# A decoder block on one core: y's row in PSUM from the first norm on, and compressed scores at a group's last unit

## The chip, the cores and the metric

The kernel runs on one core of a Trainium2 chip. The metric is the device time of one execution in microseconds; a kernel's time is the median of its runs. TensorE (PE) multiplies matrices, VectorE (DVE) and GpSimd (POOL) work element by element, ScalarE (ACT) applies functions and copies, SyncE (SP) and POOL start transfers (DMA). SBUF is the memory on the chip that all of them read; PSUM is the smaller one, in banks of 512 float32 words a partition, into which PE writes and from which DVE and ACT read.

## The reference

One layer of a decoder for 256 tokens (T) of width 2048 (D), in float32:

```python
h = x @ w_in                                     # q, 6 groups of kv columns, gates, conv columns
o_nsa  = nsa_group(q, ...)                       # 16 heads in 4 groups, head size 64
o_conv = conformer_conv_group(conv_ab, ...)      # 31 taps, norm, silu
mix = concatenate([o_nsa, o_conv], -1) @ w_out
x   = layer_norm(DN_ALPHA * x + mix, ln1_g, ln1_b)
x   = layer_norm(DN_ALPHA * x + peer_ffn(x, ...), ln2_g, ln2_b)
```

`nsa_group` adds three attentions with a gate each: over 15 compressed blocks of keys (32 tokens each, 16 apart), over selected blocks of 64 tokens (with 256 tokens there are 4 blocks, and up to 16 would be taken, so it is causal attention), and over a window of 512 (causal attention again, with keys of its own). All have a bias by distance.

`peer_ffn` computes, for each token and each of 8 heads, two score rows `s1` and `s2` over 128 keys, takes the best 16 of each, the best 16 of their 256 sums, and with those 16 experts out of 16384 the sum of softmax weight x gelu(y . u_e) x v_e:

```python
h = gelu(einsum('btd,bthkd->bthk', yb, u_tab[eidx]))
out = einsum('bthk,bthkd->btd', softmax(top) * h, v_tab[eidx])
```

## The kernel before

**Matmuls in three.** A float32 product is made of three matmuls on halves of the numbers: `hi` is the operand rounded by an ACT copy (L234), `lo` = operand - hi is a subtraction on DVE or POOL (L252), and `mm3` (L290 to L293) adds up x_hi w_hi, x_hi w_lo and x_lo w_hi, so that in the profile a weight block stands for rows of L291, L292 and L293. Weights come in pieces of 2048 columns a partition (`raw`, four buffers), each split in two halves (`hi57_0` is the first half of piece 57).

**Stages, by the time in the trace.** Up to 200 us the input projection, the convolution and the compression of keys. From 200 to 375 us the attention, beside the last query columns (`pq1` to `pq3`, one piece of `w_in` for each group of heads) and the output mix. From 375 to 405 us the first norm, whose result is `y`. From 405 to 505 us the wq stage: the router's matmuls `pwq0` to `pwq7`, a head each (four weight halves, 96 matmuls of 256 columns), with the keys' scores (`ps`), the search for the best 16 and the first ten experts. From 505 to 980 us the stage of the first dense pass: PE multiplies y with a table `u` of all experts in the lower columns (`ut` are transposes, `hp` the products), while POOL gathers (L1163) the upper 1024 columns of the chosen rows of `u` one expert for 128 tokens at a time, and DVE takes their dot product with y's upper row (`dot`, L1174). Then comes a stage of masks, from 1145 us on the v table in the same manner, and the last norm.

**What sets the order around the attention.** The order on each engine is written out by a planner. `run` (L268) issues the pieces' matmuls and moves a `clock` by a hand-made cost for each. Generators wait in `streams`; after every block of matmuls `advance` steps those whose time has come. The attention is one such generator. It goes over 16 units `u` (two heads of a group `g = u // 4` by 128 query tokens); `per` is 4. For a unit it issues `scores` (L776; `s01` and `s11` are heads 0 and 1, query tokens 128 to 255), then ACT's exponentials (`powers`, L801), the normalisation by DVE (`weigh`, L809 to L813), transposes by PE (`turn`, L824; `t00`, `t10`) with a copy by ACT (L827), and the sum over the values (`combine`), each in the round of a later unit. The compressed scores of a group (`compressed`, L714: matmuls `cs`, DVE's `csb`, transposes `ct`) run as a side generator: for group 0 ahead of the loop, for group g + 1 in the round of the first unit of group g (L901: `if u % per == 0`), which waits there for the flag `q{g+1}`, set when `pq{g+1}` is complete. Four times in each round `share` (L872) says when to go on: a list of `goals` holds, for each step, how much of the matmul work that was left at the start is to be spent by then.

**Where things lie around the first norm.** PSUM holds 8 banks. The pool `psa` has the accumulators with the tags a0 to a3, `psb` the tags S, T and o. `acc_tile` (L189) hands out accumulators by turns over four banks, or over two while the flags say so (then a2 and a3 serve `turn_tile`, L198, for the attention's transposes). In the wq stage accumulators turn over all four. y's upper row `yg` lies in SBUF. After the wq stage `apsum.close()` gives up `psa` and `psb`, and a pool `psy` takes two banks for `yp`, into which ACT copies `yg` for tokens 0 to 127 (L1447). `dot` multiplies with `yg` until then and with `yp` from then on (`yrow`). The ten dots in the wq stage therefore read `yg`. The first three tiles of `ut` are made in the wq stage (`u_split(n, True)`, L1225) in banks of the accumulators.

On POOL the wq stage's queue is, over and over: four subtractions `lo` of 128 x 1024 (L252), then a few gathers.

## Time and profile before

| | |
|---|---|
| median of 3 runs | 1660.19 us (1659.75 to 1663.21) |
| the profiled execution | 1663.05 us |
| its span in the trace | 1661.3 us |
| PE's mean granted clock in it | 0.992 |
| busy: PE, DVE, POOL, ACT | 98%, 87%, 55%, 49% |
| weight loads (PEld) | 90% |
| transfers | 475.19 MB, 286 GB/s over the span |

The span runs from the first to the last instruction; what lies around it is 1.75 us in this execution. The profile names a group of instructions by line, engine, operation, output <- input (buffer numbers left out) and how often (x). In a view by order of time a row is start, duration, engine, line and names, and a bracket gives the time that the engine stood still ahead of it and what ended that. In a view by stretches the count behind each busy time is the number of instructions. A granted clock of 1.00 is full speed of PE, 0.50 half of it.

### The profile page before, as it was taken

The page shows a single profiled execution, that of the slowest core. Times are in us where ns is not written, and L with a number is a line of the kernel's source. Part 1 is how long each engine was busy: PE and PEld are TensorE (multiplying, and loading weights), DVE is VectorE, ACT ScalarE, POOL GpSimd, SP SyncE. Part 2 cuts the span into 40 slices and gives each one's busy share as a digit, 9 for nine tenths or more (in the row PEclk, how much of TensorE's full clock was granted, in tenths as well). Part 3 has the DMA queues.
Part 4 walks back from the last instruction along what each step waited for, and adds up shares of the span by engine and source line. Part 5 has one row for each costly group of instructions (what it writes and reads, how often), then busy time and mean ns, then how long its engine had stood idle before and what let it go on. Part 6 is the DMA issues. An engine that isn't in the chain of part 4 may idle for free.

```text
span 1661.3 us, 30634 instructions
## 1 busy us (share of the span) xinstructions
PE 1621.6 (98%) x11627; PEld 1501.5 (90%) x11627; DVE 1449.5 (87%) x2651; ACT 813.4 (49%) x1261; POOL 909.0 (55%) x662
## 2 busy tenths in 40 slices
PE   9999999999999999999999999989999999999996
PEld 9998988988989999999999997878888888888885
DVE  6999668756799999999999879878898999989998
ACT  4445756544424444444444546867444444444442
POOL 1875000064783333333333347848887887778883
PEclk9999999999999999999999999999999999999998
DMA  9774535365648999999999988765999999999997
GB/s 290 234 232 130 173 102 179 110 232 191 228 159 313 349 350 354 349 351 346 350 349 355 358 314 268 244 217 169 332 358 357 352 358 349 356 347 359 363 355 260
DMA packets 178348, 475.19 MB, mean 286 GB/s; under 512 B 18304, under 2 KB 86424, under 8 KB 177944
## 3 DMA queue, kind: packets, MB, share of 16 engines
q1 hardware_dynamic: 117188, 253.62, 45.0%
q0 software_dynamic: 57488, 218.66, 35.9%
q8 instruction: 91, 1.49, 0.4%
q10 hardware_dynamic: 3524, 0.95, 0.3%
q14 instruction: 57, 0.47, 0.1%
HBM read 468.32 MB, written 4.85 MB: 285 GB/s over the span
## 4 chain that ended last, share of the span: by engine, by line
PE 61%; DVE 17%; DMA 13%; ACT 4%; issue 3%; POOL 1%; SPq 0%; POOLq 0%; DVEq 0%; ACTq 0%
DMA vr<-in_peer_v_dram 11%; PE hp L293 7%; PE hp L291 7%; PE hp L292 7%; PE ut L1231 6%; PE bank L1635 3%; PE bank L1682 3%; DVE gu L1174 3%; DVE vl L1744 3%; ACT vh L1743 3%; DVE gacc L1710 2%; PE f L292 2%; PE f L293 2%; PE f L291 2%; DVE taps L485 2%
## 5 line engine op out<-in xcount | busy, mean ns | idle before, releaser
L1705 POOL DMA_INDIRECT gv<-in_peer_v_dram,e x256 | 399.5, 1560 | 98.8 <-DVE gacc L1710 52.5
L1163 POOL DMA_INDIRECT gu<-in_peer_u_dram,eu x206 | 195.8, 951 | 311.7 <-DVE gu L1174 229.6
L291 PE MATMUL hp<-yh,uh 128*128 128x256 f32 x1024 | 310.4, 303 | 0.4 <-ACT W L1482 0.3
L1743 ACT ACTIVATE vh<-vr 128x1408 fp32r<-128x1408 f32 x127 | 175.6, 1382 | 276.1 <-DVE gacc L1710 241.5
L293 PE MATMUL hp<-yh,ul 128*128 128x256 f32 x1024 | 290.2, 283 | 0.9 <-DVE ul L1235 0.9
L292 PE MATMUL hp<-yl,uh 128*128 128x256 f32 x1024 | 289.2, 282 | 0.0
L292 PE MATMUL f<-vl,wh 128*128 128x512 f32 (+1 forms) x768 | 288.2, 375 | 1.0 <-DVE vl L1744 1.0
L293 PE MATMUL f<-vh,wl 128*128 128x512 f32 (+1 forms) x768 | 287.8, 375 | 1.0 <-DVE wl L1733 1.0
L291 PE MATMUL f<-vh,wh 128*128 128x512 f32 (+1 forms) x768 | 288.1, 375 | 0.0
L1234 ACT ACTIVATE uh<-ut 128x512 fp32r<-128x512 f32 x256 | 152.8, 598 | 254.7 <-PE ut L1231 210.1
L252 POOL TENSOR_TENSOR lo<-raw,hi 128x1024 fp32r<-128x1024 f32 (+1 forms) x84 | 189.1, 2268 | 134.7 <-ACT hi L234 128.5
L1744 DVE TENSOR_TENSOR vl<-vr,vh 128x1408 fp32r<-128x1408 f32 x127 | 206.3, 1625 | 43.2 <-ACT vh L1743 38.9
L1174 DVE SCALAR_TENSOR_TENSOR gu<-gu,yp 128x1024 f32<-128x1024 f32 x196 | 232.6, 1212 | 0.4 <-ACT yp L1457 0.2
L234 ACT ACTIVATE hi<-raw 128x1024 fp32r<-128x1024 f32 (+1 forms) x137 | 141.4, 1036 | 146.3 <-PE pwq L292 30.2
L1710 DVE SCALAR_TENSOR_TENSOR gacc<-gv,hv,gacc 128x640 f32<-128x640 f32 x246 | 206.7, 879 | 3.9 <-DMA gv<-in_peer_v_dram,e 3.8
L293 PEld LDWEIGHTS hp<-yh,ul 128*128 128x128 f32 x1024 | 195.5, 191 | 1.4 <-DVE ul L1235 1.1
L291 PEld LDWEIGHTS hp<-yh,uh 128*128 128x128 f32 x1024 | 196.0, 191 | 0.8 <-ACT W L1482 0.8
L292 PEld LDWEIGHTS hp<-yl,uh 128*128 128x128 f32 x1024 | 196.5, 192 | 0.0
L1235 DVE TENSOR_TENSOR ul<-ut,uh 128x512 fp32r<-128x512 f32 x256 | 166.8, 681 | 14.9 <-ACT uh L1234 12.9
L292 PEld LDWEIGHTS f<-vl,wh 128*128 128x128 f32 x768 | 148.5, 193 | 23.3 <-DVE vl L1744 2.5
L293 PEld LDWEIGHTS f<-vh,wl 128*128 128x128 f32 x768 | 148.6, 194 | 21.2 <-DVE wl L1733 1.4
L291 PEld LDWEIGHTS f<-vh,wh 128*128 128x128 f32 x768 | 148.5, 193 | 20.6
(410 smaller groups left out, 3556.2 us busy)
## 6 DMA issues: line engine op xcount, KB each, us to landing
vr<-in_peer_v_dram SPq DMA_DIRECT2D x128, 704.0 KB
ur<-in_peer_u_dram SPq DMA_DIRECT2D x128, 512.0 KB
raw<-in_w_in_dram SPq DMA_DIRECT2D x32, 1024.0 KB
raw<-in_w_out_dram SPq DMA_DIRECT2D x16, 1024.0 KB
raw<-in_peer_wq_dram SPq DMA_DIRECT2D x15, 1024.0 KB
gv<-in_peer_v_dram,e POOLq DMA_INDIRECT x256
gu<-in_peer_u_dram,eu POOLq DMA_INDIRECT x206
raw<-in_w_in_dram SPq DMA_DIRECT2D x4, 608.0 KB
```

Of the source, the lines that this page charges most:

```text
L252: e.tensor_tensor(lo[:, a:b], src[:, a:b], hi[:, a:b].bitcast(F32), op=OP.subtract)
L291: nc.tensor.matmul(acc, lhsT=ah, rhs=bh, start=start, stop=False)
L292: nc.tensor.matmul(acc, lhsT=ah, rhs=bl, start=False, stop=False)
L293: nc.tensor.matmul(acc, lhsT=al, rhs=bh, start=False, stop=stop)
L1163: nc.gpsimd.indirect_dma_start(out=gt, out_offset=None, in_=ug, in_offset=bass.IndirectOffsetOnAxis(ap=fl(eu, tt)[:, c:c + 1], axis=0))
L1174: nc.vector.scalar_tensor_tensor(gt, gt, 1.0, yr, op0=OP.mult, op1=OP.mult, accum_out=hv[:, tt, c:c + 1])
L1234: nc.scalar.activation(uh, pt, AF.Copy)
L1235: nc.vector.tensor_tensor(ul, pt, uh.bitcast(F32), op=OP.subtract)
L1705: nc.gpsimd.indirect_dma_start(out=gvs[j, tt], out_offset=None, in_=v_tab, in_offset=bass.IndirectOffsetOnAxis(ap=fl(e4, tt)[:, j:j + 1], ...
L1710: engine.scalar_tensor_tensor(gacc[:, tt], gvs.pop((j, tt)), wv[:, tt, j:j + 1], gacc[:, tt], op0=OP.mult, op1=OP.add)
L1743: nc.scalar.activation(vh, src[:, s], AF.Copy)
L1744: (nc.gpsimd if early else nc.vector).tensor_tensor(vl, src[:, s], vh.bitcast(F32), op=OP.subtract)
```

## The change

It has two parts.

In the **attention**, the side generator of the next group's compressed scores starts in the round of a group's last unit (u = 3, 7, 11) where it started in that of its first (u = 0, 4, 8), and it waits for the queries' copy (`box["qt"]`) besides the flag. `share` no longer takes from a list made at the start: at each step it shares what is left of the matmul work at that time by the weights still to come.

In **PSUM**, the accumulators a2 and a3 move to a pool of their own on the right side (`psc`), which is closed when the first norm is done. `psy` and `yp` are opened there at once, with the copy and the setting of `yrow`, which were behind the wq stage. With the flag "norm" set, the wq stage's accumulators turn over two banks, and its three early `ut` tiles take the tags T, o and T of `psb`.

```diff
+    cpsum = ctx.enter_context(ExitStack())
+    psc = cpsum.enter_context(tc.tile_pool(name="psc", bufs=1, space=PSUM, side="right"))
...
     def acc_tile(name):
-        two = "kv" in flags and "attn" not in flags
+        two = ("kv" in flags and "attn" not in flags) or "norm" in flags
...
-        return psa.tile([P, 512], F32, name=name, tag=f"a{n}")
+        return (psa if n < 2 else psc).tile([P, 512], F32, name=name, tag=f"a{n}")
 
     def turn_tile(name):
-        pool, tag = ((psb, "T"), (psa, "a2"), (psa, "a3"))[turns["t"] % 3]
+        pool, tag = ((psb, "T"), (psc, "a2"), (psc, "a3"))[turns["t"] % 3]
...
-        goals, due = [], spent
         weights = [WEND if k >= n - 1 else 1.0 for k in range(n + 2) for _ in range(4)]
-        for w in weights:
-            due += left(nphase + 1) * w / sum(weights)
-            goals.append(due)
+        owed = [spent]
 
         def share():
-            due = goals.pop(0)
-            if due > spent:
-                yield clock + due - spent
+            owed[0] = max(owed[0], spent - 1.0)
+            owed[0] += (left(nphase + 1) + spent - owed[0]) * weights[0] / sum(weights)
+            weights.pop(0)
+            if owed[0] > spent:
+                yield clock + owed[0] - spent
...
-            if u % per == 0 and u < n - per:
+            if u % per == per - 1 and u < n - 1:
                 yield from wait(f"q{u // per + 1}")
+                yield box["qt"]
                 assert side is None
                 side = compressed(u // per + 1)
...
-        pt = acc_tile(f"ut{j}_{b}") if early else psu.tile([P, 512], F32, name=f"ut{j}_{b}", tag="ut", bufs=4)
+        pt = psb.tile([P, 512], F32, name=f"ut{j}_{b}", tag="ToT"[n], bufs=1) if early else psu.tile([P, 512], F32, name=f"ut{j}_{b}", tag="ut", bufs=4)
...
         nc.sync.dma_start(y_dram[:, :, UD:], yg)
+        flags.add("norm")
+        cpsum.close()
+        psy = yps.enter_context(tc.tile_pool(name="psy", bufs=1, space=PSUM, side="right", reuse_waits="tile"))
+        yp = psy.tile([P, UG], F32, name="yp")
+        nc.scalar.activation(yp, yg[:, 0], AF.Copy)
+        yrow["tt"], yrow["at"] = 0, yp
         yh, yl = yt
         q0 = wq_scores(0)
...
     apsum.close()
     psu = ups.enter_context(tc.tile_pool(name="psu", bufs=2, space=PSUM, reuse_waits="tile"))
-    psy = yps.enter_context(tc.tile_pool(name="psy", bufs=1, space=PSUM, side="right", reuse_waits="tile"))
-    yp = psy.tile([P, UG], F32, name="yp")
-    nc.scalar.activation(yp, yg[:, 0], AF.Copy)
-    yrow["tt"], yrow["at"] = 0, yp
```

What this does to the order of the instructions shows at two places. The first is PE at the attention's first units. `pq1` and `pq2` are the next groups' queries, `cs10` and `cs11` the compressed scores of group 1, `s01` and `s11` the scores of unit 1, `s20` and `s30` those of unit 2, `t00` and `t10` the transposes of unit 0; numbers behind a name are the tile's. Before:

```order
L293 MATMUL pq1_2584<-xh8_93,lo33_1_2630 128x256
...
L293 MATMUL pq2_2753<-xh8_92,lo34_0_2689 128x256
L730 MATMUL cs10_2762<-kc_2147,qT1_2751 128x15
...
L730 MATMUL cs11_2763<-kc_2147,qT1_2751 128x15
L783 MATMUL s01_2783<-kds_1942,qT0_2436 128x256
...
L783 MATMUL s11_2784<-kdw_2126,qT0_2436 128x256
L824 MATMUL t00_2794<-ident_84,sc0_2668 128x128 x2
L824 MATMUL t10_2803<-ident_84,sc0_2668 128x128 x2
L783 MATMUL s20_2818<-kds_1942,qT0_2436 128x128
```

And with the change (lines from 107 on lie two further down):

```order
L295 MATMUL pq1_2587<-xh8_96,lo33_0_2576 128x256
L785 MATMUL s01_2726<-kds_1945,qT0_2439 128x256
...
L785 MATMUL s11_2727<-kdw_2129,qT0_2439 128x256
L293 MATMUL pq1_2587<-xh8_96,hi33_1_2578 128x256
...
L826 MATMUL t00_2749<-ident_87,sc0_2671 128x128 x2
...
L295 MATMUL pq1_2587<-xh8_96,lo33_1_2633 128x256
L826 MATMUL t10_2770<-ident_87,sc0_2671 128x128 x2
...
L295 MATMUL pq2_2787<-xh8_95,lo34_0_2692 128x256
L785 MATMUL s20_2800<-kds_1945,qT0_2439 128x128
```

Unit 1's scores and unit 0's transposes moved into the second half of `pq1`: six of its matmuls stand between s11 and t00, twelve between t00 and t10, and its last six behind t10, ahead of `pq2`. The matmuls of cs10 and cs11 are no longer there; they come about a hundred rows further down, behind unit 3.

The second place is ACT at the end of the first norm. `yh8` is half of y's transpose, `hi57_0` a weight half, `pq` the copy of the first head's router result out of `pwq0`. Before:

```order
L234 ACTIVATE hi56_1_4756<-raw56_4500 128x1024
L1318 ACTIVATE yh8_4720<-yt30_4774 128x4x128
L1318 ACTIVATE yh8_4720<-yt31_4781 128x4x128
L234 ACTIVATE hi57_0_4800<-raw57_4533 128x1024
L1184 ACTIVATE pq_4829<-pwq0_4664 128x512
L234 ACTIVATE hi57_1_4831<-raw57_4533 128x1024
```

And with the change:

```order
L236 ACTIVATE hi56_1_4759<-raw56_4503 128x1024
L1320 ACTIVATE yh8_4723<-yt30_4777 128x4x128
L1320 ACTIVATE yh8_4723<-yt31_4784 128x4x128
L236 ACTIVATE hi57_0_4803<-raw57_4536 128x1024
L1395 ACTIVATE yp_4836<-yg_4312 128x1024
L1186 ACTIVATE pq_4838<-pwq0_4667 128x512
L236 ACTIVATE hi57_1_4840<-raw57_4536 128x1024
```

The copy of y's row stands between `hi57_0` and the first head's copy. On DVE the ten dots of the wq stage stand where they stood, with `yp` in the place of `yg`; the order on POOL and SP is the same as before.

## The prediction

> **What bounds the kernel now.** I read the page first, then the busy times by stage.

> ```profile
> span 1661.3 us, 30634 instructions
> PE 1621.6 (98%) x11627; PEld 1501.5 (90%) x11627; DVE 1449.5 (87%) x2651; ACT 813.4 (49%) x1261; POOL 909.0 (55%) x662
> ```

> PE is busy for 98% of the span, so a change can only win where PE stands still or runs slowly. The stages say where that is (columns: stretch, its length, busy us of PE, PEld, DVE, ACT and POOL, PE's granted clock, DMA share, GB/s):

> ```profile
> 200.00:232.00 32.00, 28.73 (x230) 25.99 (x229) 19.32 (x50) 18.73 (x45) 0.00 (x0) 0.89 0.41 127
> 232.00:375.00 143.00, 142.42 (x1174) 127.06 (x1173) 100.33 (x197) 81.12 (x188) 31.82 (x19) 1.00 0.50 165
> ...
> 455.00:505.00 50.00, 45.21 (x360) 44.17 (x360) 48.31 (x151) 15.96 (x26) 37.65 (x22) 0.97 0.48 159
> 505.00:980.00 475.00, 473.77 (x4038) 472.80 (x4037) 456.60 (x980) 220.61 (x385) 177.84 (x191) 1.00 0.96 349
> ```

> Two of these stages lose time: the start of the attention (200 to 232 us, 3.3 us idle, clock 0.89) and the second half of the wq stage (455 to 505 us, 4.8 us idle, clock 0.97). The change touches both. The long expert stage behind them is full on PE (473.8 of 475 us), so what the first 505 us lose or win should reach the end unchanged. Next, PE in order of time in the two stretches; the bracket is the idle time before the row and what ended it:

> ```profile
> 216.67 1.07 PE L730 MATMUL cs<-kc,qT 64*128 64x15 f32 x16 [0.86 <-ACT qT L678]
> 219.41 0.92 PE L824 MATMUL t<-ident,sc 128*128 128x128 f32 x4 [0.71 <-DVE sc L813]
> 220.59 0.97 PE L783 MATMUL s<-kds,qT 64*128 64x128 f32 x3 [0.26 <-DVE sc L790]
> 225.35 1.12 PE L824 MATMUL t<-ident,sc 128*128 128x128 f32 x4 [0.82 <-DVE sc L813]
> ```
> ```profile
> 458.87 0.39 PE L293 MATMUL pwq<-yh,lo 128*128 128x256 f32 x1 [0.53 <-POOL lo L252]
> 473.85 0.39 PE L293 MATMUL pwq<-yh,lo 128*128 128x256 f32 x1 [2.33 <-POOL lo L252]
> 488.79 0.39 PE L293 MATMUL pwq<-yh,lo 128*128 128x256 f32 x1 [0.80 <-POOL lo L252]
> 503.36 0.44 PE L1231 MATMUL ut<-ident,ur 128*128 128x128 f32 x2 [0.82 <-DVE ul L1235]
> ```

> And the granted clock just behind those waits, in stretches cut at its steps:

> ```profile
> 215.30:222.10 6.80, 4.86 (x43) 3.52 (x42) 4.16 (x13) 2.00 (x4) 0.00 (x0) 1.00 0.39 135
> 222.10:228.90 6.80, 5.98 (x29) 5.68 (x29) 5.09 (x15) 4.28 (x17) 0.00 (x0) 0.50 0.00 0
> 228.90:235.70 6.80, 6.80 (x62) 5.82 (x61) 3.47 (x9) 2.72 (x6) 0.00 (x0) 1.00 0.50 157
> ...
> 474.70:478.10 3.40, 3.40 (x19) 3.40 (x18) 3.40 (x1) 0.00 (x0) 3.40 (x2) 0.50 0.09 34
> ...
> 983.30:986.70 3.40, 2.70 (x18) 1.62 (x19) 2.42 (x5) 2.69 (x5) 2.53 (x3) 1.00 0.74 205
> 986.70:990.10 3.40, 3.40 (x19) 2.74 (x18) 1.25 (x2) 0.74 (x2) 2.48 (x4) 0.50 0.89 296
> 385.90:389.30 3.40, 1.66 (x13) 1.48 (x13) 3.12 (x7) 2.18 (x6) 0.00 (x0) 1.00 0.15 60
> 389.30:392.70 3.40, 3.06 (x26) 2.92 (x26) 1.99 (x4) 3.35 (x6) 1.80 (x1) 1.00 0.36 139
> ```

> After each of the two groups of waits the clock is halved, for 6.8 and for 3.4 us. A stall of PE here costs twice: the wait, then slow matmuls.

> **Part 1, the attention's order.** In before, unit 0 waits for the whole of pq1 and then puts the next group's scores (cs), unit 1's scores (s01, s11) and unit 0's transposes (t00, t10) on PE in one lump, each waiting for what the last one started. That is the first fence of PE rows above: 0.86 + 0.71 + 0.26 + 0.82 = 2.65 us of waits. In the change unit 1 starts while pq1 is still running, with pq1's matmuls between its steps, and cs1 comes after unit 3, when qT1 has long been there. Unit 0's softmax is done well before pq1 ends (ACT's last read of its sums, and PE's last pq1 matmul):

> ```profile
> 210.72 0.19 ACT L801 ACTIVATION_READ_ACCUMULATOR sc<-sc,st 128x1 f32 x1
> ```
> ```profile
> 215.53 0.28 PE L293 MATMUL pq<-xh,lo 128*128 128x256 f32 x1
> ```

> So 4.6 us of pq1 matmuls are left in which DVE can normalise unit 0 (L809 to L813) and PE can start unit 1, and the order puts them there: s01 behind pq1's matmuls on lo33_0, then six of pq1's, t00, twelve more, t10 and the last six. I take 2.65 us off and put 0.5 us back for waits at the new places, so -2.15. Bounds: -2.65 if nothing waits there, 0 if the same waits come back.

> The half clock from 222.1 to 228.9 us holds 5.98 us of PE work, which at full clock would take 2.99: -3.0. Bounds -3.0 and 0, because no row proves that the waits caused it; I take the full value since it follows the densest group of PE waits in the stage and nothing else is odd there. [...]

> The new shares only spread the same attention work over the same matmuls; 232 to 375 us is 142.4 of 143 us busy, so I cost them at nothing, the cover being the mixa and pq matmuls. If that cover fails, it is the rival on DVE below.

> **Part 2, y's row in PSUM.** Ten dot products in the wq stage read yg in SBUF; now they read yp in PSUM. DVE's long ones and POOL's rows there:

> ```profile
> 459.83 7.12 DVE L1174 SCALAR_TENSOR_TENSOR gu<-gu,yg 128x1024 f32<-128x1024 f32 x1
> ...
> 473.93 7.95 DVE L1174 SCALAR_TENSOR_TENSOR gu<-gu,yg 128x1024 f32<-128x1024 f32 x1
> ...
> 488.85 5.64 DVE L1174 SCALAR_TENSOR_TENSOR gu<-gu,yg 128x1024 f32<-128x1024 f32 x1
> ```
> ```profile
> 456.42 9.45 POOL L252 TENSOR_TENSOR lo<-raw,hi 128x1024 fp32r<-128x1024 f32 x4
> 467.24 1.70 POOL L1163 DMA_INDIRECT gu<-in_peer_u_dram,eu  x1 [1.37 <-DVE gu L1174]
> ...
> 471.43 9.36 POOL L252 TENSOR_TENSOR lo<-raw,hi 128x1024 fp32r<-128x1024 f32 x4
> 486.36 7.03 POOL L252 TENSOR_TENSOR lo<-raw,hi 128x1024 fp32r<-128x1024 f32 x3
> ```
> ```profile
> L1163 POOL DMA_INDIRECT gu<-in_peer_u_dram,eu x14: 934/944/1697, 437.0 to 504.9; - x14
> ```

> Each long dot begins inside a block of POOL subtractions and ends 1.0 us after it (456.42 + 9.45 = 465.87; the dot ends at 466.95): DVE is locked out until POOL is done. POOL then waits 1.37 us for that dot, and its next gather takes 1.70 us where 0.94 is the median. With yp this does not happen:

> ```profile
> L1174 DVE SCALAR_TENSOR_TENSOR gu<-gu,yp x196: 1204/1210/1222, 509.0 to 998.1; 128x1024 f32<-128x1024 f32 x196
> L1174 DVE SCALAR_TENSOR_TENSOR spare<-spare,yp x17: 1207/1209/1217, 1004.0 to 1098.5; 128x1024 f32<-128x1024 f32 x17
> ```
> ```profile
> 1048.81 2.38 POOL L1794 TENSOR_TENSOR spare<-spare,morel 128x1024 f32<-128x1024 f32 x1
> ```

> No dot on yp takes over 1222 ns, though POOL multiplies in the same stretch. So DVE gains 7.12 + 7.95 + 5.64 - 3 x 1.21 = 17.1 us, but off the path. What PE sees is POOL's blocks starting earlier. The block at 456.42 is unchanged, so the wait of 0.53 stays. Then the next gather starts at 465.87 + 0.3 (my allowance for the issue) instead of 467.24, and is 1.70 - 0.94 = 0.76 us shorter: the next block starts 1.1 + 0.7 = 1.8 us earlier, and the wait of 2.33 falls to about 0.5. From then on POOL needs three gathers, 1.25 us each with what lies between them ((471.43 - 467.24 - 1.70) / 2), and four subtractions (9.4), 13.2 us a cycle, against PE's 12.4 (488.79 - 473.85 = 14.94, less its 0.80 of wait and 1.7 of half clock), so a wait near 0.8 stays at the third place. Together -1.8 us (bounds -3.7 and 0). The half clock from 474.7 to 478.1, 3.40 us of PE work, goes with the 2.33: -1.7 (bounds -1.7 and 0). The ul that PE waits 0.82 for at 503.36 stands on DVE behind the dots; the last dot is 5.64 - 1.21 = 4.4 us shorter: -0.8 (bounds -0.8 and 0).

> The copy of y to yp moves from 503.5 us to the front of the wq stage, on ACT between these two rows:

> ```profile
> 402.60 1.06 ACT L234 ACTIVATE hi<-raw 128x1024 fp32r<-128x1024 f32 x1 [0.77 <-PE pwq L292]
> 405.67 0.60 ACT L1184 ACTIVATE pq<-pwq 128x512 f32<-128x512 f32 x1 [2.01 <-PE pwq L293]
> ```

> ACT idles for 2.01 us there and the copy takes about 1.06, as the row above it for the same shape: free; without that idle it would delay the pq copy, and the ps matmuls behind it, by 1.06 us. Its two banks held accumulators that y itself is made from, so they are read before the copy's operand is there. The wq accumulators now take turns in two banks instead of four; each is emptied by a copy of 0.60 us right after its last matmul, and a head's matmuls (12.4 us) lie between two uses of a bank: nothing.

> **The sum**, against the profiled execution (1663.05 us, span 1661.3; 2.9 above the median of 1660.19): 1663.05 - 2.15 - 3.0 - 1.8 - 1.7 - 0.8 = 1653.6. That is 6.6 us below the median, 0.4%. If the other two runs stand 2.9 us lower for a reason that has nothing to do with these stalls, the whole 9.45 us come off the median and the result is 1650.7; I take the value reckoned from the profiled run, since a halved clock less is just what could make the others shorter. A measurement of this kernel can tell about 0.2% (3.3 us) from no change.

> **Rivals.** *The waits go, the half clock does not* (it moves to other matmuls): only 2.15 + 1.8 + 0.8 = 4.75 us are won, 1658.3. For it: the clock is also halved at 986.7, where PE hardly waits. 13%. [...]

> *The attention keeps its loss*: the lump is only moved to units 3, 7 and 11. Then part 2 alone is left, 4.3 us: 1658.8. Against it: 232 to 375 us, with cs2 and cs3 in it, is idle for 0.6 us in all. 8%.

> *Slower, through DVE at the compressed scores.* DVE already stands before csb:

> ```profile
> DVE csb L735 <- PE cs L730: 10.0, 3, 3.5
> ```
> ```profile
> 224.94 1.14 DVE L813 TENSOR_SCALAR sc<-sc,st 128x256 f32<-128x256 f32 x4
> ...
> 229.66 0.87 DVE L813 TENSOR_SCALAR sc<-sc,st 128x128 f32<-128x128 f32 x4
> ```

> In the change, what queues behind csb is L813 of a group's last unit, on 256 columns where it was 128: 1.14 - 0.87 = 0.27 us more, and PE's matmuls of the next unit are the short kind and hide less (an estimate of 0.4 us). If DVE's slack there is zero, PE waits 3 x 0.67 = 2.0 us at the three places, and it decides once the clock halves behind each: 3 x 3.0 more. Attention's 5.65 us of loss become 11.0, part 2 still wins 4.3: 1663.05 + 5.35 - 4.3 = 1664.1. Against it: DVE is busy for 100.33 of the 143 us there, so that it mostly has slack. 4%.

> *The lead is lost in the expert stage*, if its DMA (0.96 busy, 349 GB/s) sets the pace and the earlier start only meets a later transfer: 1660 to 1663. Against it: PE is 473.8 of 475 us busy there. 5%.

> **How the numbers follow.** Forecast 70%, rivals 13, 8, 4 and 5%. The likeliest is 1653.6. The range goes down to 1648.0 (1650.7, less 1.9 if all POOL waits go and 0.8 for the spread of the runs) and up to 1660.0, which takes in the first two rivals and the lower end of the last. Faster by over 0.2% means below 1656.9: the forecast and a part of the first two rivals, 0.75; same 0.20 (the rest of these, and the lost lead); slower 0.05.

> **What would show it.** Right: no dot over 1.25 us before 505 us; no PE wait on L813 or qT between 210 and 230; clock 1.00 there and around 470; the wq stage's largest lo wait below 1 us; the expert stage as long as before. Wrong: halved stretches of the same total length elsewhere, PE waits on L813 behind cs1 to cs3, or a longer expert stage.

## The result and the profile after

The changed kernel takes 1653.36 us (median of 6 runs, 1650.69 to 1654.46) where the kernel before, now with 6 runs, takes 1660.97 us. The ratio is 0.9946 with a 95% interval of 0.9935 to 0.9957: between 7 and 11 us faster. The profiled execution took 1653.22 us with a span of 1651.4 us, 9.8 us less than the profiled one of before; that one lay 2.1 us above its median, so the two traces show a little more than the medians, which lie 7.6 us apart.

The same stretches as in the prediction, in the changed kernel (columns: stretch, its length, busy us of PE, PEld, DVE, ACT and POOL, PE's granted clock, DMA share, GB/s):

```profile
200.00:232.00 32.00, 31.50 (x292) 28.97 (x292) 21.32 (x46) 21.99 (x55) 0.00 (x0) 1.00 0.46 145
232.00:375.00 143.00, 141.33 (x1140) 125.89 (x1139) 101.74 (x205) 78.55 (x179) 32.53 (x19) 1.00 0.51 169
455.00:505.00 50.00, 48.82 (x409) 48.18 (x408) 35.52 (x135) 16.60 (x30) 34.67 (x24) 1.00 0.62 207
505.00:980.00 475.00, 472.22 (x4004) 469.18 (x4003) 454.84 (x974) 220.53 (x385) 179.53 (x192) 1.00 0.96 347
```

PE's idle time fell from 3.3 to 0.5 us in the first stretch and from 4.8 to 1.2 us in the third, and the clock is 1.00 in both. The second stretch is the one that got worse, from 0.6 to 1.7 us idle. PE's waits in order of time say why, and what is left of the third:

```profile
264.56 0.63 PE L826 MATMUL t<-ident,sc 128*128 128x128 f32 x4 [1.28 <-DVE sc L815]
...
453.34 0.39 PE L295 MATMUL pwq<-yh,lo 128*128 128x256 f32 x1 [0.52 <-POOL lo L254]
466.42 0.39 PE L295 MATMUL pwq<-yh,lo 128*128 128x256 f32 x1 [0.43 <-POOL lo L254]
479.50 0.39 PE L295 MATMUL pwq<-yh,lo 128*128 128x256 f32 x1 [0.43 <-POOL lo L254]
```

The four waits of unit 0 (2.65 us) are gone. One of 1.28 us is new, at the compressed scores of group 2, and a short one of 0.38 us stands at those of group 3 (292.94 us); another of 0.50 us, which the kernel before had at 284.37 us, is gone. Of the lo waits of 0.53, 2.33 and 0.80 us there are 0.52, 0.43 and 0.43 left. The dots of the wq stage, as a group (ns, shortest, median, longest), and POOL in order of time:

```profile
L1176 DVE SCALAR_TENSOR_TENSOR gu<-gu,yp x14: 1197/1216/1222, 448.4 to 504.1; 128x1024 f32<-128x1024 f32 x14
```
```profile
449.92 0.95 POOL L1165 DMA_INDIRECT gu<-in_peer_u_dram,eu  x1 [5.38 <-DVE vf L1059]
450.88 9.46 POOL L254 TENSOR_TENSOR lo<-raw,hi 128x1024 fp32r<-128x1024 f32 x4
460.50 0.95 POOL L1165 DMA_INDIRECT gu<-in_peer_u_dram,eu  x1 [0.16 <-DVE scr L1066]
...
463.96 9.46 POOL L254 TENSOR_TENSOR lo<-raw,hi 128x1024 fp32r<-128x1024 f32 x4
```

No dot takes over 1222 ns, and the gather behind a block of subtractions starts 0.16 us after it, where it started 1.37 us after it and took 1.70 us.

Where the time went shows best in the places at which PE reaches certain matmuls. This table was made from the traces (start of the last matmul of the attention, `po`; of the first and the last `hp`, which bound the dense pass; and of the last `bank` matmul, with which the stage of the masks ends; us). The rows below the second are the runs told of further down.

| kernel | last po | first hp | last hp | last bank | span |
|---|---|---|---|---|---|
| before | 345.4 | 500.9 | 983.0 | 1150.1 | 1661.3 |
| after | 339.9 | 491.6 | 973.5 | 1140.0 | 1651.4 |
| after, once more | 341.5 | 493.1 | 974.4 | 1141.1 | 1651.7 |
| attention part alone | 341.4 | 496.9 | 979.0 | 1144.8 | 1655.5 |
| PSUM part alone | 344.5 | 496.3 | 978.1 | 1146.0 | 1655.6 |
| old shares | 339.7 | 491.4 | 972.5 | 1136.3 | 1646.3 |
| dots from SBUF | 341.4 | 496.8 | 978.0 | 1145.1 | 1655.1 |
| three lumps | 339.8 | 501.5 | 983.3 | 1151.7 | 1660.4 |
| nine pieces | 341.4 | 500.7 | 983.4 | 1149.6 | 1659.8 |
| scores behind the norm | 337.9 | 489.5 | 970.6 | 1141.6 | 1652.5 |
| later gather | 339.6 | 489.1 | 970.2 | 1139.0 | 1649.0 |
| both later | 337.5 | 487.0 | 968.1 | 1132.8 | 1643.3 |

From before to after: 5.5 us by the end of the attention, 3.8 us more by the first hp, and 0.2 us in the dense pass (482.1 and 481.9 us long). The dense pass is 481.1 to 482.7 us long in all twelve traces. The stage behind it varies between 163.8 and 171.0 us, without any pattern that follows the changes; a single trace is therefore compared up to 970 us only.

### The profile page after: what moved, and what is told of

Same layout as the page of the kernel before. It is cut to its first block, busy times and chain, and to the rows that moved or that the text cites. A ratio compares the mean times of both kernels' runs of the same rounds, so it can differ in the third digit from the quotient of the medians.

```text
span 1651.4 us, 30625 instructions
## 1 busy us (share of the span) xinstructions
PE 1614.3 (98%) x11627; PEld 1497.0 (91%) x11627; DVE 1433.6 (87%) x2651; ACT 814.3 (49%) x1261; POOL 905.3 (55%) x662
## 4 chain that ended last, share of the span: by engine, by line
PE 56%; DMA 18%; DVE 14%; issue 5%; ACT 4%; POOL 2%; SPq 0%; POOLq 0%; DVEq 0%; ACTq 0%
DMA vr<-in_peer_v_dram 13%; PE hp L293 7%; PE hp L295 7%; PE hp L294 7%; PE ut L1233 6%; DVE vl L1748 3%; DVE gacc L1714 3%; PE bank L1639 3%; ACT vh L1747 3%; PE bank L1686 2%; DMA gv<-in_peer_v_dram,e 2%; PE pwq L295 2%; DVE taps L487 2%; PE pwq L294 2%; PE pwq L293 2%
## 5 line engine op out<-in xcount | busy, mean ns | idle before, releaser
L293 PE MATMUL hp<-yh,uh 128*128 128x256 f32 x1024 | 310.4, 303 | 0.4 <-ACT W L1486 0.3
L293 PE MATMUL f<-vh,wh 128*128 128x512 f32 (+1 forms) x768 | 288.1, 375 | 0.0
L1176 DVE SCALAR_TENSOR_TENSOR gu<-gu,yp 128x1024 f32<-128x1024 f32 x206 | 244.8, 1212 | 7.7 <-DMA gu<-in_peer_u_dram,eu 7.3
L293 PEld LDWEIGHTS hp<-yh,uh 128*128 128x128 f32 x1024 | 196.0, 191 | 0.8 <-ACT W L1486 0.8
L293 PEld LDWEIGHTS f<-vh,wh 128*128 128x128 f32 x768 | 148.5, 193 | 20.7
```

What stands on the lines that cost most here:

```text
L293: nc.tensor.matmul(acc, lhsT=ah, rhs=bh, start=start, stop=False)
L1176: nc.vector.scalar_tensor_tensor(gt, gt, 1.0, yr, op0=OP.mult, op1=OP.mult, accum_out=hv[:, tt, c:c + 1])
```

## Experiments

Each ratio is to the kernel before, run beside the kernel in question. Its median there was 1660.84 us for the first four kernels below, 1662.74 us for the changed kernel once more and for both later steps, and 1663.06 us for the others, so times of different groups are best compared by their ratios.

**The attention part alone.** Edit: the kernel before with the two hunks of the attention.

```diff
-            if u % per == 0 and u < n - per:
+            if u % per == per - 1 and u < n - 1:
                 yield from wait(f"q{u // per + 1}")
+                yield box["qt"]
```

> The kernel before with the attention part alone (compressed scores at a group's last unit, shares worked out anew). My theory: the two parts are independent; PE's waits around unit 0 and the halved clock behind them go, so about 5.5 us of the 9.8 us by which the profiled span fell belong to this part: the first wq matmul starts about 5.5 us earlier than before, the wq stage keeps its lo waits of 0.5, 2.3 and 0.8 us, and the median is 1655 to 1657 (before 1661.0). Rival, the halved clock only moves: 2.5 us, 1658.5. Rival, the gain comes only with both parts together: 1660 to 1661.

Measured: 1657.25 us, ratio 0.9972 (0.9961 to 0.9983), some 4.7 us by the ratio; the median lies just above the 1655 to 1657 that were expected. The attention ends 4.1 us earlier, and from there to the first hp it takes 155.5 us, as before (155.4): the wq stage is untouched, lo waits of 3.8 us in all and the halved clock included. What is missing against the 5.5 us is a halved clock at 265 us (below): in this trace a halving did come back, at another place. The two parts are independent.

**The PSUM part alone.** Edit: the changed kernel with the goals and the place of the compressed scores of before.

> The kernel before with the PSUM part alone (yp from the first norm on, two accumulator banks, early ut tiles in other banks). My theory: the attention keeps its waits (2.65 us) and its half clock; the wq stage shortens by 3.8 us (POOL's lo waits 0.53, 2.33, 0.80 to about 0.55 each, the half clock at 475 us gone, ul's 0.8 gone): 1657.0 to 1658.0. Rival, half the gain of the wq stage is only that the attention ended earlier (another phase of the clock's windows): 1659 to 1660.

Measured: 1657.73 us, ratio 0.9980 (0.9967 to 0.9992), some 3.3 us. From the last po to the first hp it takes 151.8 us, as in the changed kernel (151.7). So the wq stage gives 3.6 to 3.8 us with either attention, and the rival that half of it came from another phase falls. But the attention, in the same order as before, ran otherwise than expected. PE in order of time at unit 0 and the windows there:

```profile
217.30 1.07 PE L732 MATMUL cs<-kc,qT 64*128 64x15 f32 x16 [0.86 <-ACT qT L680]
220.04 0.92 PE L826 MATMUL t<-ident,sc 128*128 128x128 f32 x4 [0.71 <-DVE sc L815]
221.23 0.97 PE L785 MATMUL s<-kds,qT 64*128 64x128 f32 x3 [0.27 <-DVE sc L792]
225.99 0.70 PE L826 MATMUL t<-ident,sc 128*128 128x128 f32 x4 [1.83 <-DVE sc L815]
```
```profile
217.74:221.15 3.41, 2.51 (x24) 1.69 (x22) 2.61 (x12) 0.69 (x2) 0.00 (x0) 1.00 0.20 67
221.15:224.57 3.42, 2.82 (x20) 2.30 (x20) 2.68 (x7) 1.51 (x7) 0.00 (x0) 1.00 0.00 0
224.57:227.98 3.41, 1.99 (x17) 1.94 (x18) 2.71 (x9) 1.44 (x5) 0.00 (x0) 1.00 0.00 0
```

The clock is never halved there, though the first three waits are the same to 0.01 us; and the fourth wait is 1.83 us where it was 0.82. The attention ends only 1.0 us earlier than in before (it also starts 0.6 us later in this trace: cs at 201.3 against 200.7). So the 6.8 us at half clock cost before about 1.6 us, and not 3.0. At half clock PE spent a part of that time on work where it otherwise waits, since DVE's normalisation (L815) is what ends last; the longer fourth wait is 1.0 us of the difference, and the rest isn't split further.

**The old shares.** Edit: the changed kernel with the list of goals.

```diff
-        owed = [spent]
+        goals, due = [], spent
...
+        for w in weights:
+            due += left(nphase + 1) * w / sum(weights)
+            goals.append(due)
```

> The changed kernel with the list of goals made at the start, as in before, and the compressed scores at the last unit. My theory: the gain of the attention comes from the move of the compressed scores, since the order around units 0 to 8 is the same with either share and differs only from group 3 on: within 1 us of the changed kernel, 1652.5 to 1654.5. Rival, the shares are what places the units: the attention loses 3 us or more of its 5.5 us, 1656 to 1658.

Measured: 1651.51 us, ratio 0.9951 (0.9937 to 0.9965), the changed kernel's within the interval; last po at 339.7 against 339.9 us. With either way of sharing the move gives the gain, so the gain of the attention is the move's, and beside it the shares do nothing that can be measured. What the new shares do without the move was not run.

**The dots from SBUF.** Edit: the changed kernel, `yrow` set only behind the wq stage.

```diff
         nc.scalar.activation(yp, yg[:, 0], AF.Copy)
-        yrow["tt"], yrow["at"] = 0, yp
         yh, yl = yt
...
     apsum.close()
+    yrow["tt"], yrow["at"] = 0, yp
```

> The changed kernel, but the ten dots of the wq stage read yg in SBUF as before; the copy to yp, the two accumulator banks and the other banks of the early ut tiles stay. My theory: the dots' operand alone carries the gain of the wq stage: three dots of 5 to 8 us come back, a lo wait of about 2.3 us, and where it falls so that the clock halves 1.7 us more: 3 to 4 us longer than the changed kernel, 1656.5 to 1657.5. Rival, it is the banks or the earlier copy (the dots' length lies beside the path): within 1 us of 1653.4.

Measured: 1657.18 us, ratio 0.9983 (0.9970 to 0.9996). DVE in order of time:

```profile
455.77 7.10 DVE L1176 SCALAR_TENSOR_TENSOR gu<-gu,yg 128x1024 f32<-128x1024 f32 x1
...
469.83 7.98 DVE L1176 SCALAR_TENSOR_TENSOR gu<-gu,yg 128x1024 f32<-128x1024 f32 x1
...
484.77 5.65 DVE L1176 SCALAR_TENSOR_TENSOR gu<-gu,yg 128x1024 f32<-128x1024 f32 x1
```

The three long dots are back to 0.03 us, and each ends 1.1 us after the end of a block of POOL's subtractions (461.77, 476.72 and 489.33 us). Last po to first hp is 155.4 us again, as in before and with the attention part alone. Up to the first hp the operand alone carries the gain of the wq stage; the early copy, the two accumulator banks and the other banks for ut cost and gain nothing there.

Just behind the first hp (496.80 us here) they do change something. PE's wait of 0.82 us for `ul` is in before and with the attention part alone, but not here, although the last dot is as long as before:

```profile
498.31 0.60 PE L1233 MATMUL ut<-ident,ur 128*128 128x128 f32 x4
```
```profile
498.58 0.67 DVE L1237 TENSOR_TENSOR ul<-ut,uh 128x512 fp32r<-128x512 f32 x1
```

This ul starts 1.8 us after the first hp, as in before (502.65 against 500.86 us), yet PE's ut no longer stands behind it. So it is the PSUM part without the operand that removes this wait, most likely the other banks of the early ut tiles; that was not run by itself.

**Delays in three lumps and in nine pieces.** Edit: the changed kernel with part of a `lo` subtracted twice on POOL ahead of the real one, once 1024 columns at each of three places, once 304 columns at each of nine.

```diff
+            if (i, s) in ((64, 1), (66, 1), (68, 1)):
+                nc.gpsimd.tensor_tensor(lo[:, :1024], src[:, :1024], hi[:, :1024].bitcast(F32), op=OP.subtract)
```

> The changed kernel with a subtraction of 128 x 1024 done twice on POOL at three places of the wq stage (lo64_1, lo66_1, lo68_1), each where PE already waits for it: 3 x 2.4 us more of PE waits, in lumps of about 3.0 us. My theory, from the traces so far: the clock halves for 3.41 us behind a window of 3.41 us in which PE stood still for 2 us or more in all, wherever the windows happen to lie; a lump of 3.0 us puts that much into one window about 2 times in 3. So 7.2 us for the waits and 2 halved windows at 1.7 us: first hp 10 to 12 us later than in the changed kernel, 1663 to 1665. [...]

> The same 7.2 us of POOL work as in the other kernel, but in nine pieces of 0.8 us, one ahead of three lo in each of the same three heads. My theory: PE waits as long in all (7 us), but no window holds 2 us of it, so the clock stays at 1.00 from 400 to 500 us: 1660 to 1661, some 3 us less than with three lumps. Rival, what halves the clock is POOL's load or the number of waits and not their density: halved windows here as well, 1663 to 1665.

Measured: 1661.27 us, ratio 0.9990 (0.9977 to 1.0003), with the lumps; 1661.98 us, 0.9994 (0.9979 to 1.0009), with the pieces. By the ratios that is some 7.3 and 8.0 us over the changed kernel: the two can't be told apart, the 3 us that I expected between them don't show, and the time with the lumps lies below the 1663 to 1665 us that I expected; the 7.2 us of waits alone would give 1653.4 + 7.2 = 1660.6. Only the clock in the traces decides. The second kernel did not do what it was made for: PE does not wait for each piece. It runs through what lies ready and then waits for POOL's whole arrears at one lo, so there are lumps here as well. By luck that made the better experiment. PE's waits in order of time, and the windows, of the kernel with nine pieces:

```profile
471.46 0.39 PE L297 MATMUL pwq<-yh,lo 128*128 128x256 f32 x1 [3.12 <-POOL lo L256]
487.23 0.58 PE L297 MATMUL pwq<-yh,lo 128*128 128x256 f32 x1 [3.12 <-POOL lo L256]
```
```profile
466.57:469.98 3.41, 1.77 (x15) 1.56 (x14) 0.56 (x1) 1.26 (x2) 3.01 (x4) 1.00 0.95 334
469.98:473.40 3.42, 1.94 (x16) 1.94 (x17) 2.93 (x5) 0.00 (x0) 3.34 (x3) 1.00 0.38 152
473.40:476.81 3.41, 3.41 (x31) 3.41 (x31) 1.72 (x12) 1.21 (x2) 3.33 (x3) 1.00 0.02 5
483.63:487.05 3.42, 0.48 (x5) 0.28 (x3) 1.23 (x3) 0.00 (x0) 3.33 (x3) 1.00 0.89 308
487.05:490.46 3.41, 3.23 (x15) 3.23 (x16) 2.46 (x4) 0.00 (x0) 3.33 (x4) 0.50 0.10 42
```

Two waits of 3.12 us. The first lies across two windows, which leaves PE 1.77 and 1.94 us busy in them, and the clock stays at 1.00. The second lies in one window, 0.48 us busy, and the next window runs at 0.50. PE's waits with the lumps:

```profile
455.63 0.58 PE L297 MATMUL pwq<-yh,lo 128*128 128x256 f32 x1 [2.94 <-POOL lo L256]
471.10 0.39 PE L297 MATMUL pwq<-yh,lo 128*128 128x256 f32 x1 [1.47 <-POOL lo L256]
486.60 0.58 PE L297 MATMUL pwq<-yh,lo 128*128 128x256 f32 x1 [2.85 <-POOL lo L256]
```
```profile
451.86:455.27 3.41, 0.83 (x7) 0.63 (x6) 3.41 (x18) 1.06 (x1) 3.33 (x2) 1.00 0.36 135
455.27:458.69 3.42, 3.06 (x14) 3.07 (x15) 2.40 (x6) 0.00 (x0) 3.42 (x3) 0.50 0.49 143
468.92:472.33 3.41, 1.94 (x16) 1.74 (x16) 2.46 (x4) 1.06 (x1) 3.41 (x2) 1.00 0.20 82
472.33:475.75 3.42, 3.42 (x31) 3.42 (x31) 0.83 (x5) 1.21 (x2) 3.42 (x3) 1.00 0.02 5
482.58:485.99 3.41, 1.16 (x10) 0.96 (x8) 2.26 (x4) 0.00 (x0) 3.33 (x2) 1.00 0.68 259
485.99:489.40 3.41, 2.81 (x13) 2.81 (x14) 1.23 (x2) 0.00 (x0) 3.41 (x3) 0.50 0.00 0
```

The wait of 2.94 us is followed by one halved window, the one of 2.85 us by two, and the one of 1.47 us by none. The first hp came 9.9 us later than in the changed kernel, for 5.9 us more of waits there. The clock stayed at 1.00 throughout in neither kernel. My theory of 2 us in one window fits the rows of both: the windows in which PE is idle for 2.58, 2.25 and 2.93 us by these rows have a clock of 0.50 behind them, those with 1.47, 1.64 and 1.48 us one of 1.00. Why the wait of 2.85 us has a second halved window behind it, the rows don't show: the first, from 485.99 us, is idle for only 0.60 us. Neither the length of the single wait (3.12 us in both cases with nine pieces) nor POOL's load (3.01 to 3.41 us in each of these six windows) explains them.

**The changed kernel once more.** No edit.

> The changed kernel once more, unaltered, on the same chip as the other kernel of this call. Every order is the same, so what differs from its first trace is only where the clock's windows lie: my theory is that the waits of PE come back to 0.1 us up to 970 us, that a wait of 1.45 us at 263 us halves the clock behind it or not (both were seen), and that the stages up to the first hp agree within 2 us; median within 0.15% of 0.9946 of before.

Measured: 1652.21 us, ratio 0.9939 (0.9921 to 0.9958). The windows around the wait of 1.28 us at 263 to 264.6 us, first in the trace from above and then in this one:

```profile
260.21:263.62 3.41, 3.07 (x47) 2.57 (x45) 1.20 (x5) 0.71 (x1) 0.00 (x0) 1.00 1.07 364
263.62:267.03 3.41, 2.47 (x22) 2.50 (x23) 3.31 (x12) 1.53 (x5) 0.00 (x0) 1.00 1.04 377
267.03:270.45 3.42, 3.42 (x34) 2.74 (x33) 3.25 (x11) 2.72 (x10) 0.00 (x0) 1.00 1.09 361
```
```profile
261.18:264.59 3.41, 2.12 (x35) 1.79 (x32) 1.70 (x9) 0.57 (x2) 0.00 (x0) 1.00 1.06 359
264.59:268.01 3.42, 3.42 (x17) 3.42 (x18) 3.38 (x8) 1.94 (x8) 0.00 (x0) 0.50 1.05 388
```

The same wait is cut in two by a window's border in the one and lies within a window in the other; the second trace halves its clock, and its last po comes 1.5 us later. The wait is not alone in its window: with the shorter gaps between matmuls beside it, PE's idle time there is about 2.4 us (measured as in the last section). Of the eight traces with this order up to 263 us, four halve (last po at 341.4 or 341.5) and four do not (339.6 to 339.9).

**The compressed scores behind the normalisation.** Edit: the changed kernel; the side generator starts at the end of a group's last round and makes its first step in the next round, behind `weigh` and `scores`.

```diff
             if u < n:
                 ready = scores(u)
+            if u % per == 0:
+                beside()
             divide()
...
-            if u % per == per - 1 and u < n - 1:
-                yield from wait(f"q{u // per + 1}")
-                yield box["qt"]
-                assert side is None
-                side = compressed(u // per + 1)
             if u >= 2:
                 combine(u - 2)
             beside()
+            if u % per == per - 1 and u < n - 1:
+                yield from wait(f"q{u // per + 1}")
+                yield box["qt"]
+                assert side is None
+                side = compressed(u // per + 1)
```

> The changed kernel, but the next group's compressed scores are begun one step later: behind the normalisation of the group's last unit and the scores of the next unit, and no longer ahead of them on DVE. In the changed kernel PE waits 1.28 us at 263 us for L815, which stands on DVE behind csb (my rival on DVE at the compressed scores). My theory: that wait and the one of about 0.5 us at 292 us go, and with them the chance of a halved clock at 265 us (seen in two of four traces with this order): mixb ends 1.5 to 2 us earlier, 1651 to 1652. Rival, DVE is the limit there in any order and another wait of the same length takes its place: 1653.4 within 1 us.

DVE in order of time in the changed kernel, where the wait of 1.28 us is:

```profile
262.76 0.35 DVE L737 TENSOR_TENSOR csb<-cs,bc 128x60 f32<-128x60 f32 x2 [2.15 <-PE cs L732]
...
264.06 1.14 DVE L815 TENSOR_SCALAR sc<-sc,st 128x256 f32<-128x256 f32 x4
```

and in this kernel:

```profile
258.45 1.14 DVE L815 TENSOR_SCALAR sc<-sc,st 128x256 f32<-128x256 f32 x4
...
263.12 0.34 DVE L737 TENSOR_TENSOR csb<-cs,bc 128x60 f32<-128x60 f32 x2
```

In the changed kernel DVE stands idle for 2.15 us until PE gets to cs, with the normalisation queued behind csb; put ahead of it, L815 runs 5.6 us earlier. PE then has no wait of over 0.25 us from 232 to 346 us, and the last po comes 2.1 us earlier, as expected. The median of 1653.93 us, ratio 0.9944 (0.9928 to 0.9960), doesn't show it: with this interval 2 us can't be told from nothing, and in the trace the stage behind the dense pass happened to be the longest of all (171.0 us).

**The fourth gather half a head later.** Edit: the changed kernel.

```diff
-                if h >= 3:
+                if h >= 3 and (h, half) != (4, 0):
                     while room() and issued < min(EGS, len(indexed) * TOPK):
```

> The changed kernel with one gather (the fourth, gu0_3) issued half a head later. In the changed kernel POOL stands still for 5.4 us ahead of it (it waits for DVE's first route and dot), and PE then waits for lo three times, 0.5 to 0.7 us each. My theory: POOL's queue is what sets the rest of the wq stage; without that stop all three lo waits go, 1.9 us by the issue gaps: first hp 1.5 to 1.9 us earlier, 1651.5. Rival, the lo waits come from POOL's rate (three gathers and four subtractions are 13.1 us a head, PE's head 12.4): only the first of them goes, 0.6 us, and 1652.8.

POOL in order of time:

```profile
434.76 11.80 POOL L254 TENSOR_TENSOR lo<-raw,hi 128x1024 fp32r<-128x1024 f32 x5
...
451.95 0.95 POOL L1165 DMA_INDIRECT gu<-in_peer_u_dram,eu  x1 [1.92 <-DVE vf L1059]
```

POOL stands still for 1.92 us ahead of that gather and not for 5.38, and PE has no lo wait left in the wq stage. Last po to first hp is 149.5 us, 2.1 us less than in the changed kernel. The time is 1652.83 us, ratio 0.9939 (0.9922 to 0.9957); it is the rival's number, but the interval takes in the changed kernel and can't decide. The trace does: all three waits are gone, so POOL's rate alone, my rival, does not make PE wait within the stage.

**Both later steps.**

> The changed kernel with both later steps: compressed scores begun behind the normalisation of a group's last unit, and the fourth gather half a head later. My theory: the two gains add up on the path (2.06 us by the end of mixb, 2.1 us in the wq stage in the single traces): first hp about 4.1 us earlier than in the changed kernel, and 1649 to 1650 where the changed kernel has 1653.4, unless halved windows in the stages behind 970 us happen to differ, which moves a single run by 1 to 3 us. Rival, a lead of the first 490 us is lost again later (the stage from 970 to 1141 us was 4.5 us longer in the trace with the first step alone): within 1 us of the changed kernel.

Measured: 1648.47 us, ratio 0.9916 (0.9898 to 0.9934), against 1652.21 us and 0.9939 of the changed kernel, run beside it. First hp comes at 487.0 us, 4.6 us before the changed kernel's. PE in its stretches:

```profile
200.00:232.00 32.00, 31.49 (x296) 28.93 (x294) 22.88 (x54) 21.80 (x55) 0.00 (x0) 1.00 0.45 140
232.00:375.00 143.00, 143.00 (x1143) 127.52 (x1142) 102.32 (x203) 77.71 (x179) 32.60 (x19) 1.00 0.51 170
...
455.00:505.00 50.00, 49.69 (x420) 49.43 (x420) 39.62 (x148) 17.86 (x32) 31.97 (x24) 1.00 0.63 218
```

The attention's second stretch is full, and the wq stage has 0.3 us idle. This kernel has the lowest time of all that ran. It beats the kernel before clearly; over the changed kernel its gain is the 4.6 us of the trace and 3.7 us by these two medians, with intervals that still overlap.

## Why the prediction was right, and where a step was not

*The sum* came out: 1653.6 forecast, 1653.36 measured. In the traces, 9.45 us forecast and 9.8 us found. By the medians the change is 7.6 us: the prediction reckoned from a profiled execution that lay 2.1 us above its median, so that the time was met to 0.3 us is partly luck. Its terms did not all come out.

*Part 1, 2.15 us of waits and 3.0 us of half clock.* The total was 5.15 and is 5.5 us, but the split was wrong. The mis-sized term is the half clock at 222 us: the step "at full clock would take 2.99: -3.0" counted the slowed matmuls as if nothing lay beside them. The PSUM kernel has the same order without the halving and gets back about 1.6 us of the 3.0, as its fourth wait grows from 0.82 to 1.83 us. The order itself was worth more than 2.15: from the PSUM kernel to the changed one, both at full clock, the attention ends 4.5 us earlier, 4.1 us when the later start is taken off. Waits of over 0.25 us account for 2.5 us of that (4.2 us in the one, 1.7 us in the other, where the prediction had put back 0.5); the rest lies in shorter gaps, whose cause the runs don't show. Too much for one term and too little for the other came to nearly the right sum, which is luck. Whether the clock halves at all depends on the execution, which the step did not know: in the second trace of the changed kernel the total is 4.0 us.

*Part 2.* From the last po to the first hp 3.8 us went. The lo waits fell by 2.3 us (1.8 forecast; the third, kept at 0.8, fell to 0.43 since PE's head takes 13.08 - 0.43 = 12.65 us and not 12.4). The other 1.5 us are the halved window, where the term had 1.7: between the second wait and the third PE took 14.94 - 0.80 = 14.14 us and now takes 12.65. These two are not separate gains, though. In both kernels the second and the third wait end when POOL is done, so POOL's cycle sets the pace: between the rows of PE that wait for lo it fell from 14.98 and 14.94 us to 13.08 twice (13.2 in the prediction), which is 3.8 us by itself. By these rows, what the halved window cost came off the wait behind it.

The reason, dots locked out by POOL's subtractions, was shown by giving the dots their SBUF operand back; that the banks and the copy cost nothing up to the first hp was shown by the same run. That run also shows that one step was wrong: the ul wait of 0.82 us went as forecast, but not because the last dot became shorter. It is gone with the long dot too. It also lies behind the first hp, in a dense pass that became only 0.2 us shorter (482.1 to 481.9 us), so that the term of 0.8 can't be found in the time.

*The shares* were costed at nothing, and beside the move they are nothing.

*Rivals.* The one on DVE at the compressed scores was real, at one place of the three with 1.28 us and at another with 0.4 us, where it was priced at 0.67 us each. PE's waits on L815 behind the compressed scores were one of the signs that the prediction named for being wrong. The rival did not decide, since unit 0's waits were larger. "DVE is busy for 100.33 of the 143 us" was a bad argument against it: DVE stood idle for 2.15 us right ahead of that wait. A mean share says nothing about an engine that works in order. The lead was not lost in the dense pass (482.1 and 481.9 us). That the attention keeps its loss fell with the attention part alone. The rival that the half clock only moves fell for the profiled pair up to 505 us (behind it there are three halved windows, at 977, 1093 and 1110 us, where before has two, at 987 and 1113 us). But half of the eight traces with the new order do have a halved window at 265 us, worth 1.5 us.

*The halved clock.* In the second trace of the changed kernel it stands behind a wait of 1.28 us, with the shorter gaps beside it, and in the kernel with nine pieces one wait of 3.12 us has none behind it; the halved stretches are 3.41 us long or a multiple (6.83 us at 222 us of before), and one order halves in four of eight traces. So the length of a single wait does not decide it in these traces. By the busy time in the prediction's rows of before, 385.9 to 389.3 us is idle for 1.74 us and is followed by a clock of 1.00, and 983.3 to 986.7 us is idle for 0.70 us and is followed by 0.50. That busy time hides gaps: by the starts of the matmuls these two windows have 2.00 and 2.18 us.

## What to carry to other kernels

Before costing an operation on DVE, see which block of POOL's subtractions runs beside it: a PSUM operand took a dot from 7.98 to 1.22 us here without any other change. When PE waits for an engine that works in order, look at what that engine waits for just ahead of the row in question, and move the work that is ready in front of it (here L815 ran 5.6 us earlier and the last po came 2.1 us earlier). And don't add a wait and the slow matmuls behind it in full: here they overlapped (6.8 us at half clock cost about 1.6 us and not 3.0), and whether the clock fell depended on the execution (four of eight traces).

## What the runs showed of the hardware

In the traces' record of the granted clock, up to 1600 us, the halved stretches of before begin at 222.119, 474.705, 986.704 and 1112.998 us; the first lasts 6.827 us, the others 3.413 us. Those of after begin at 977.006, 1093.059 and 1110.126 us and last 3.413 us each. The distances between these beginnings are 74, 150 and 37 times 3.41333 us in the one and 34 and 5 times in the other, to within 1 ns. The windows in this document are steps of that length, counted off from such a beginning in the same trace; they lie elsewhere in each execution (a border at 263.62 us in the first trace of the changed kernel, at 264.59 us in the second). PE's idle time in each window can be measured from the starts of the matmuls: from each gap between two starts, take off the median gap behind a matmul of that shape in the same trace, and sum up what is left. This finds gaps that the profile's busy time hides (2.18 us and not 0.70 us at 983.3 us of before). Counted over the twelve traces of this case, for windows at full clock from 20 to 1600 us:

```
idle in the window (us)   windows   next window at half clock
under 1.8                 5436      0
1.8 to 2.0                19        0
2.0 to 2.1                19        1
2.1 to 2.2                8         3
over 2.2                  35        29
```

Also unexpected: delays put on POOL in nine pieces reached PE as one wait a head, 1.40, 3.12 and 3.12 us long. How the work was spread on POOL said little here about how the waits were spread.
